# HGRN2 head outputs turned by VectorE through DRAM instead of by TensorE

## The chip, the cores and the metric

The kernel runs on one core of a Trainium2 chip. The metric is device microseconds of one execution, lower is better. The engines are named as the profile names them: PE (TensorE), DVE (VectorE), ACT (ScalarE), POOL (GpSimd) and SP (SyncE, which only issues transfers here); PEld is the load of PE's stationary operand.

## The reference

One layer over 2112 tokens: 2048 of a prompt and 64 of a second, decoded sequence with a state of its own. D is 1024, there are 8 heads of 128. Cut to what matters:

```python
h = rms_norm(x, g_pre)
vA, bA, cA, zA, q, f, iv, zB, gA, gB = split_cols(h @ w_in)        # ten products of 1024
yA = (silu(zA) * bA * causal_conv3(cA * vA, conv_w)) @ w_a_out     # path A
fg = lb + (1 - lb) * sigmoid(f); kk = 1 - fg; qq = silu(q) * 128 ** -0.5
# path B: per head, chunks of 64 tokens, b = cumsum(log fg) within the chunk
att = causal(qe @ ke.T)                  # qe = q exp(b - ref), ke = k exp(ref - b)
o = att @ v + (q * exp(b)) @ S
S = exp(b_last) * S + (k * exp(b_last - b)).T @ v
o = o * rsqrt(mean(o * o) + EPS)         # over the head's 128 channels
yB = ((o * g_onorm) * silu(zB)) @ w_b_out
x = x + rms_norm((sigmoid(gA) * yA + sigmoid(gB) * yB) @ w_o, g_post)
x = x + (p @ w_ple_proj) * sigmoid(rms_norm(x, g_ple) @ w_ple_gate)
```

The mean over a head's channels is along a row of `o` when tokens lie on the partitions; the product with `silu(zB)` and `w_b_out` needs channels on the partitions. So the normalised outputs have to be turned, 128x128 at a time. So have keys and values, which the products over tokens need with tokens on the partitions.

## The kernel before, in words

The tokens are worked through in three blocks of 768, 704 and 640. Block 1 holds the decoded sequence as a half group of 64 tokens. In a block the order is: path B (eight heads), path A, the merge of both, the product with `w_o`, the norm, the last gate. Activations stand with channels on the partitions and tokens on the free axis. Activations and weights are split into a high and a low part in a rounded format, so that a product is three matmuls for each piece of 128 of the contraction (L442, L443, L444).

The large products go through `sgroup` (L427): two output tiles of 128 channels at once, in seven products of a Strassen-Winograd scheme over half the contraction and half the tokens (`PRODUCTS`). Its weights are the blocks of `w_in` and their sums S1 to S4. Block 0 makes these sums (`combined`, additions L352), splits each into halves (ACT casts the high one, DVE subtracts for the low one, L226) and stores what later blocks read again. For weights that only later stages of block 0 need, `prepare_sums` (L364) makes sums ahead, in pieces: load on POOL's queue, an addition on DVE (`keep`, L390), a store on POOL's queue (L393), and the low half (L226, stored by L387).

`sgroup` calls `hook()` once after each of its seven products. `hooks` is a list of steps of other work; each call takes the next entry, which may be None. That sets how work is interleaved: `head_prep` (L936) runs two `sgroup`s for one head, the forget gate with the values and then the output gate zB with the queries, that is 14 hooks, and in them run the attention steps of the head before. In block 0 every head after the first is followed by one `sgroup` of the gates gA and gB (`next(fills)`), which makes 21 hooks a head; in blocks 1 and 2 only one head is.

Within `head_prep` the values (all blocks) and, in blocks 1 and 2, the keys are turned by a round trip. `turned` (L1045): DVE transposes 32x32 squares (L1049), POOL's queue writes the tile to DRAM (L1051). `in_rows` (L1053): POOL's queue reads it back in an order that completes the turn (L1056), and for keys POOL copies it once more into plain columns (L1061).

`head_attn` (L1064) is a generator with four steps for a part of a head, up to four pairs of chunks (a pair is a group of 128 tokens). A block of 768 has the parts 4 + 2, one of 640 has 4 + 1, block 1 has the half group beside these:
1. in block 0, and for the half group, PE transposes the keys (L1093) into PSUM and ACT copies them out (L1095); then the scores on PE (L1121) and their masking on DVE;
2. products of keys and values for the state, and the states;
3. the outputs on PE (L1161, L1163), their squares and the norm, to a tile `on`;
4. PE transposes the pairs back (L1179), and one DVE instruction a part multiplies them, out of PSUM, with `g_onorm` and the gate tile `z` (L1181), in place in `z`.

Then `keep_z` (L1191) stores `z` to DRAM on POOL's queue; the merge reads it later. The query tile's product with the decay factors, `queries`, is on POOL in block 0 (L1017) and on DVE else (L1016). Evictions of `sgroup` stand on ACT (L456) and DVE (L462, L471, L490). Each engine runs its instructions in the order in which they are issued, and so does each queue's issuing engine. Tiles of 128 x up to 770 come from one pool, `ring`, of 48 buffers.

Of the kernel before, what the change touches and what calls it, by code (L numbers as in the profile page):

```python
# [93 lines left out]
def hybrid_step(  # L94
# [266 lines left out]
            total("S4", a12, s2, ALU.subtract)  # L361
            return out

    def prepare_sums(firsts, shared=False, pieces=False):  # L364

        def second(i1):
            return i1 + (KH if i1 >= W_A else 1)  # L370

        def tile_of(dt=F32):
            return rt(4 * P, dt).rearrange("p (k c) -> p k c", c=P)

        def load(i1):
# [12 lines left out]

        def keep(name, i1, out, x, y, op):
            V.tensor_tensor(out, x, y, op)  # L390
# [542 lines left out]
    def chunks(t):  # L933
        return t.rearrange("p (c t) -> p c t", t=CH)

    def head_prep(bl, hc, hd, first, hs):  # L936
        n, npair = bl["n"], bl["npair"]
        nch, np1 = n // CH, npair * P
        sf, vt = rt(), rt()
# [29 lines left out]
        def scaled(after):  # L969


            with tc.issue_after(after):
                if first:
                    A.activation(sf, sf, AF.Identity, bias=omlb[:, hd : hd + 1], scale=nomlb[:, hd : hd + 1])
                A.activation(r, ref.rearrange("p c o -> p (c o)"), AF.Exp)
                A.activation(eq, lg, AF.Exp)
                A.activation(lg, lg, AF.Exp, scale=-1.0)
            V.tensor_tensor(f[:, 1:nch], r[:, 1:nch], chunks(eq)[:, : nch - 1, CH - 1], ALU.mult)
            V.tensor_copy(f[:, 0:1], r[:, 0:1])
            for g in bl["groups"]:  # L980
                if g["sample"]:
                    c = g["off"] // CH
                    V.tensor_copy(f[:, c : c + 1], r[:, c : c + 1])
            f1, f2 = f[:, 0 : 2 * npair : 2], f[:, 1 : 2 * npair : 2]

            ka3 = ka.rearrange("p (g t) -> p g t", t=CH)
            more = npair - 2 * SWAP
            for lo, hi, to in (
                (0, SWAP, ka3[:, more + 1 :: 2, :]),
                (SWAP, 2 * SWAP, ka3[:, more : npair - 1 : 2, :]),  # L990
                (2 * SWAP, npair, ka3[:, :more, :]),
            ):
                own = slice(2 * lo, 2 * hi, 2)
                V.tensor_tensor(to, chunks(sf)[:, own, :], chunks(lg)[:, own, :], ALU.mult)
                scale = f2[:, lo:hi].unsqueeze(2).to_broadcast([P, hi - lo, CH])
                place = slice(2 * lo + (hi <= SWAP), 2 * hi, 2)
                V.tensor_tensor(chunks(kb)[:, place, :], to, scale, ALU.mult)
            for lo, hi in ((0, SWAP), (SWAP, npair)):
                seconds, place = slice(2 * lo + 1, 2 * hi, 2), slice(2 * lo + (hi > SWAP), 2 * hi, 2)
                V.tensor_tensor(chunks(kb)[:, place, :], chunks(sf)[:, seconds, :], chunks(lg)[:, seconds, :], ALU.mult)  # L1000
            if not first:
                wrote.append(turned("tk", kb, b, npair))
            if nch % 2:
                end = slice(nch - 1, nch)
                V.tensor_tensor(chunks(kb)[:, end, :], chunks(sf)[:, end, :], chunks(lg)[:, end, :], ALU.mult)
            V.tensor_tensor(f2, f2, f1, ALU.mult)
# [12 lines left out]
        def sink_q(c, h, x, y):  # L1019
# [4 lines left out]
            else:  # L1024
                v = whole(x, y)
                A.activation(half(z, h), v, AF.Sigmoid)
                V.tensor_tensor(half(z, h), v, half(z, h), ALU.mult)

        with behind_all(summed[-1] if first and hd == 0 else ()):
            sgroup(ZB * 8 + hd, QQ * 8 + hd, hc, sink_q, first, mid=scaled, free=first)  # L1030
        with tc.issue_after(freed[0]) if first else nullcontext():
            queries()
        with behind_all([*wrote, *powers]):
            by_token = [in_rows(kind, npair) for kind in (("tv",) if first else ("tv", "tk"))][::-1]
        return dict(
            eq=eq, f=f, ka=ka, kb=kb, qe=qe, qx=qx, vt=vt, z=z, by_token=by_token,
            more=npair - 2 * SWAP, first=first, last=bl["last"], carry=None,
        )

    def cols3(t, nt):  # L1040
# [9 lines left out]
        turning[kind] = dram.tile([P, n], F32, tag=f"{kind}{npair}", name=nm(kind), bufs=2)  # L1050
        return G.dma_start(turning[kind], out[:, :n]).ins  # L1051

    def in_rows(kind, npair):  # L1053

        t = rt(npair * P)
        G.dma_start(t.rearrange("q (i c) -> q i c", i=4), turning[kind].rearrange("(i b) (j c) -> (b j) i c", i=4, j=4))  # L1056
        t = t.rearrange("q (i g a) -> q g i a", i=4, a=32)
        if kind == "tv":
            return t
        kt = rt(npair * P)  # L1060
        G.tensor_copy(kt.rearrange("q (g i a) -> q g i a", i=4, a=32), t)  # L1061
# [2 lines left out]
    def head_attn(ip, gs, d, hd):  # L1064
# [93 lines left out]
        with placed():  # L1158
            for i, g in enumerate(gs):
                dst = p_o[:, i * P : i * P + P]  # L1160
                T.matmul(dst, att[:, i, :], v[:, i], start=True, stop=prevs[i] is None)  # L1161
                if prevs[i] is not None:
                    T.matmul(dst, cols(d["qx"], g), prevs[i], start=False, stop=True)  # L1163
        on = tile3(2)
        ms = small.tile([P, 4], F32, tag="ms", name=nm("ms"))
        po3 = cols3(p_o, nt)
        if d["first"]:
# [10 lines left out]
            for i in range(nt):  # L1178
                T.transpose(p_t[:, i * P : i * P + P], on[:, i, :], ident)  # L1179
        c = slice(o0, o0 + n)  # L1180
        V.scalar_tensor_tensor(z[:, c], p_t[:, P - ln : P - ln + n], g_on[:, hd : hd + 1], z[:, c], ALU.mult, ALU.mult)  # L1181
        yield

    def each(steps):
        for step in steps:
            step()

    def path_b(bl, hc, first, kept, fills, hs, lead_sums=None):


        def keep_z(hd, z):  # L1191
            kept["o", hd] = spill("o", hd)
            G.dma_start(kept["o", hd], z)

        for hd in range(NH):
            d = head_prep(bl, hc, hd, first, hs)
            if hd > 0 if first else hd == KH + 1:
                next(fills, None)
            assert not hooks
            lead = first and hd == 0  # L1200
            attn = [head_attn(i, gs, d, hd) for i, gs in enumerate(bl["parts"])]
            hooks.extend([None] * (1 + lead if first else 2))
            if not first:
                pairs, one = attn[:2], attn[2:]
                piece = lead_sums and [partial(next, lead_sums, None)]
                for steps in (pairs[:1], pairs[1:], one, one, pairs, one, pairs, piece, one, pairs[:1], pairs[1:]):
                    hooks.append(partial(each, [s if callable(s) else partial(next, s) for s in steps]) if steps else None)
            for step in range(4 * first):
                hooks.extend(partial(next, g) for g in attn)

                hooks.extend([None] * (0 if step == 3 else 3 - len(attn) - (lead and step == 0) + (step == 2)))
            hooks.append(partial(keep_z, hd, d["z"]))
            if first:
                piece = partial(next, lead_sums, None)
                hooks.extend([piece, None, piece, None, piece] if hd else [None, piece])
        if first:
            hooks.extend([None, None, None, piece] * 12)


    parked = []  # L1220
# [375 lines left out]
    for bi, bl in enumerate(blocks):  # L1596
# [145 lines left out]
```

## Time and profile before

| | |
|---|---|
| time, median of three runs | 2563.28 us (2561.38, 2563.28, 2568.24) |
| the profiled execution | 2561.54 us, of which the span of the profile is 2559.8 |
| granted clock of PE | 0.999 |
| ACT, share of the span | 1485.7 us, 58% |
| POOL, share of the span | 451.0 us, 18% |
| the commonest transfer: weights of 256 KB, issued by SP | 577 times, 4.5 us to landing |

The page gives the busy time of each engine, the span in 40 slices, the transfers by kind, the chain of work that ended last, and groups of instructions by line. L12 is line 12 of the kernel; lines of the kernel before are meant unless it is said otherwise. Many instructions run one behind another with overlap, so a duration is not the time that one more instruction costs; that is read from the distance of starts in the timeline.

### The profile page before, as it was taken

What the parts mean: (1) busy time and instruction counts of PE and PEld (TensorE: products, weight loads), DVE (VectorE), ACT (ScalarE), POOL (GpSimd) and SP (SyncE); (2) the same over time, 40 slices, a digit from 0 to 9 for tenths busy, and PEclk for the clock granted to TensorE, in tenths of its full rate; (3) what the DMA queues carried; (4) which work ended last, traced back from release to release, by engine and by line L of the source; (5) the groups of instructions that cost most, each with busy time, mean ns of one, the idle gap of its engine ahead of it and who ended that gap; (6) DMA issues with size and microseconds to landing.
All of it is one profiled execution on the core that took longest, in us unless ns stands there. A gap on an engine that the chain in (4) does not pass through costs nothing.

```text
span 2559.8 us, 47168 instructions
## 1 busy us (share of the span) xinstructions
PE 2540.1 (99%) x16150; PEld 2525.1 (99%) x16150; DVE 1778.2 (69%) x3541; ACT 1485.7 (58%) x2880; POOL 451.0 (18%) x781
## 2 busy tenths in 40 slices
PE   9999999999999999999999999999999999999999
PEld 9999999999999999999999999999999999999998
DVE  7888888898868775576574556987446655336967
ACT  6666666554453664466565555567456665446675
POOL 2122122220022021122221221102112111001011
PEclk9999999999999999999999999999999999999999
DMA  8789888998797888988888999989998898999986
GB/s 330 256 272 321 275 285 287 329 368 300 257 345 249 266 315 263 304 279 285 309 271 290 342 392 314 324 292 334 296 306 299 294 317 288 298 299 324 338 271 202
DMA packets 368400, 767.11 MB, mean 300 GB/s; under 512 B 45398, under 2 KB 50192, under 8 KB 368160
## 3 DMA queue, kind: packets, MB, share of 16 engines
q1 hardware_dynamic: 321696, 582.69, 67.2%
q0 software_dynamic: 46464, 181.41, 19.8%
q8 instruction: 127, 2.08, 0.3%
q14 instruction: 113, 0.93, 0.1%
HBM read 557.07 MB, written 206.85 MB: 298 GB/s over the span
## 4 chain that ended last, share of the span: by engine, by line
PE 76%; issue 3%; DVE 3%; DMA 3%; ACT 1%; POOL 0%; SPq 0%; DVEq 0%; ACTq 0%; POOLq 0%
PE pg L442 16%; PE pg L444 16%; PE pg L443 16%; PE pg L594 4%; PE pg L593 4%; PE pg L595 4%; PE pg L633 3%; PE pg L632 3%; PE pg L631 3%; DMA lo<-low 1%; DMA raw<-w_blk 1%; PE pa L1121 1%; PE pa L1161 1%; PE pa L1163 1%; PE pa L1107 1%
## 5 line engine op out<-in xcount | busy, mean ns | idle before, releaser
L442 PE MATMUL pg<-r,hi 128*128 128x320 f32 (+2 forms) x3304 | 1084.0, 328 | 0.0
L443 PE MATMUL pg<-r,hi 128*128 128x320 f32 (+2 forms) x3304 | 1067.7, 323 | 0.0
L444 PE MATMUL pg<-r,lo 128*128 128x384 f32 (+2 forms) x2356 | 768.8, 326 | 4.3 <-DMA lo<-low 4.1
L273 ACT CAST hi<-raw 128x512 fp32r<-128x512 f32 x730 | 449.9, 619 | 493.5 <-PE pg L443 185.6
L442 PEld LDWEIGHTS pg<-r,hi 128*128 128x128 f32 x3304 | 621.8, 188 | 0.7
L443 PEld LDWEIGHTS pg<-r,hi 128*128 128x128 f32 x3304 | 622.2, 188 | 0.0
L444 PEld LDWEIGHTS pg<-r,lo 128*128 128x128 f32 x2356 | 442.8, 188 | 6.0 <-DMA lo<-low 5.6
L444 PE MATMUL pg<-r,s 128*128 128x352 f32 (+1 forms) x948 | 300.0, 316 | 1.7 <-DMA s<-low 1.7
L594 PE MATMUL pg<-r,hi 128*128 128x320 f32 (+2 forms) x864 | 277.5, 322 | 0.4 <-DVE r L226 0.2
L593 PE MATMUL pg<-r,hi 128*128 128x320 f32 (+2 forms) x864 | 274.9, 322 | 0.0
L226 ACT CAST hi<-raw 128x512 fp32r<-128x512 f32 x252 | 155.4, 620 | 168.7 <-PE pg L443 47.6
L226 DVE TENSOR_TENSOR r<-r,r 128x320 fp32r<-128x320 f32 (+7 forms) x354 | 208.5, 608 | 50.9 <-ACT r L226 49.7
L226 DVE TENSOR_TENSOR lo<-raw,hi 128x512 fp32r<-128x512 f32 x231 | 160.3, 696 | 81.7 <-ACT hi L226 78.5
L226 ACT CAST r<-r 128x320 fp32r<-128x320 f32 (+7 forms) x354 | 185.3, 557 | 49.4 <-DVE r L390 8.2
L595 PE MATMUL pg<-r,lo 128*128 128x352 f32 (+2 forms) x564 | 180.9, 321 | 0.0
L444 PEld LDWEIGHTS pg<-r,s 128*128 128x128 f32 x948 | 178.8, 189 | 2.2 <-DMA s<-low 2.2
L226 ACT CAST hi<-s 128x512 fp32r<-128x512 f32 x156 | 96.5, 619 | 130.7 <-PE pg L443 101.9
L632 PE MATMUL pg<-r,hi 128*128 128x384 f32 (+2 forms) x512 | 167.1, 327 | 0.2 <-DVE r L226 0.2
L631 PE MATMUL pg<-r,hi 128*128 128x384 f32 (+2 forms) x512 | 165.9, 327 | 0.2 <-ACT hi L273 0.2
L594 PEld LDWEIGHTS pg<-r,hi 128*128 128x128 f32 x864 | 162.1, 188 | 2.2 <-DVE r L226 1.6
L593 PEld LDWEIGHTS pg<-r,hi 128*128 128x128 f32 x864 | 161.3, 188 | 1.4 <-ACT r L226 0.7
L456 ACT COPY hf<-pg 128x352 f32<-128x352 f32 (+2 forms) x354 | 157.2, 446 | 1.0 <-PE pg L444 0.6
(396 smaller groups left out, 4109.4 us busy)
## 6 DMA issues: line engine op xcount, KB each, us to landing
raw<-w_blk SPq DMA_DIRECT2D x577, 256.0 KB, 4.5
raw<-S SPq DMA_DIRECT2D x444, 256.0 KB, 4.4
lo<-low SPq DMA_DIRECT2D x422, 256.0 KB, 4.3
s<-low SPq DMA_DIRECT2D x308, 256.0 KB, 4.4
low<-lo SPq DMA_DIRECT2D x271, 256.0 KB, 4.0
S<-s SPq DMA_DIRECT2D x152, 256.0 KB, 3.8
low<-r POOLq DMA_DIRECT2D x54, 256.0 KB, 5.1
r<-w_blk POOLq DMA_DIRECT2D x52, 256.0 KB, 6.6
```

Of the source, the lines that this page charges most:

```text
L226: return A.copy(hi, src).ins, V.tensor_tensor(lo, src, hi.bitcast(F32), ALU.subtract).ins
L273: A.copy(hi, raw)
L442: add(hi[:, k, :], xhi, start=start and k == 0, stop=False)
L443: add(hi[:, k, :], xlo, start=False, stop=False)
L444: last[0] = add(lo[:, k, :], xhi, start=False, stop=k == KH - 1).ins
L456: copied = A.copy(got[n], ps[bank])
L593: add(hi[:, k, :], xhi, start=start and k == 0, stop=False)
L594: add(hi[:, k, :], xlo, start=False, stop=False)
L595: last[0] = add(lo[:, k, :], xhi, start=False, stop=k == KH - 1).ins
L631: T.matmul(ps, hi[:, k % 4, :], xhi[:, c], start=k == ks[0], stop=False)
L632: T.matmul(ps, hi[:, k % 4, :], xlo[:, c], start=False, stop=False)
L633: last[0] = T.matmul(ps, lo[:, k % 4, :], xhi[:, c], start=False, stop=k == ks[-1]).ins
```

## The change

In four parts.

1. The normalised outputs of whole pairs, in all blocks, no longer go through PE and PSUM. They are written to a tile `on` of the whole head; `turn_o` transposes it on DVE into the head's `kb` tile and writes it to DRAM, `read_o` reads it back into `on`, and `scale_o` multiplies it into `z`: in block 0 four DVE instructions of 192 columns with `g_onorm`, in blocks 1 and 2 one product of 640. There `g_onorm` is multiplied into `z` when `z` is made (`sink_q`). The half group of block 1 is still transposed on PE. In blocks 1 and 2 the read stands ahead of the keys' read in POOL's queue.
2. Block 0's keys are turned by `turned` and `in_rows` as in the other blocks; the read and POOL's copy run at the fourth hook of the gates' `sgroup` (`read_k`), for the first head at the end of `head_prep`.
3. The additions of the sums made ahead during block 0's path B run on POOL (`adder=G`): 24 of 128x512.
4. The hooks are laid out by numbered slots (`slots`, `at`) that may reach into the next head's: in blocks 1 and 2 `scale_o` and `keep_z` stand at slot 21, where a head has 14 slots (21 with a gates' `sgroup`).

In the built programs TensorE has 15523 matmuls before and 15347 after.

```diff
-    def prepare_sums(firsts, shared=False, pieces=False):
+    def prepare_sums(firsts, shared=False, pieces=False, adder=V):
...
         def keep(name, i1, out, x, y, op):
-            V.tensor_tensor(out, x, y, op)
+            adder.tensor_tensor(out, x, y, op)
...
-    def head_prep(bl, hc, hd, first, hs):
+    def head_prep(bl, hc, hd, first, hs, before):
...
-            if not first:
-                wrote.append(turned("tk", kb, b, npair))
+            wrote.append(turned("tk", kb, b, npair))
...
-                V.tensor_tensor(half(z, h), v, half(z, h), ALU.mult)
+                V.scalar_tensor_tensor(half(z, h), v, g_on[:, hd : hd + 1], half(z, h), ALU.mult, ALU.mult)
...
-            by_token = [in_rows(kind, npair) for kind in (("tv",) if first else ("tv", "tk"))][::-1]
+            by_token = [in_rows("tv", npair)]
+            if before is not None and not first:
+                before["ot"] = in_rows("to", npair, before["on"])
+            if not first or before is None:
+                by_token.insert(0, in_rows("tk", npair))
...
-    def in_rows(kind, npair):
+    def in_rows(kind, npair, t=None):
-        t = rt(npair * P)
+        t = rt(npair * P) if t is None else t
...
-        on = tile3(2)
+        if not single:
+            d["on"] = rt(d["npair"] * P) if d["on"] is None else d["on"]
+            on = cols3(d["on"][:, o0:], nt)
+        else:
+            on = tile3(2)
...
-        V.scalar_tensor_tensor(z[:, c], p_t[:, P - ln : P - ln + n], g_on[:, hd : hd + 1], z[:, c], ALU.mult, ALU.mult)
+        V.tensor_tensor(z[:, c], p_t[:, P - ln : P - ln + n], z[:, c], ALU.mult)
...
+    def read_k(d):
+        d["by_token"].insert(0, in_rows("tk", d["npair"]))
+    def turn_o(d):
+        turned("to", d["on"], d["kb"], d["npair"])
+    def read_o(d):
+        if "ot" not in d:
+            d["ot"] = in_rows("to", d["npair"], d["on"])
+    def scale_o(d, hd):
+        z = d["z"][:, : d["npair"] * P].rearrange("q (g i a) -> q g i a", i=4, a=32)
+        if d["first"]:
+            for i in range(4):
+                V.scalar_tensor_tensor(z[:, :, i], d["ot"][:, :, i], g_on[:, hd : hd + 1], z[:, :, i], ALU.mult, ALU.mult)
+        else:
+            V.tensor_tensor(z, d["ot"], z, ALU.mult)
...
+        slots, base, d = {}, 0, None
         for hd in range(NH):
-            d = head_prep(bl, hc, hd, first, hs)
+            d = head_prep(bl, hc, hd, first, hs, d)
+            if len(d["by_token"]) == 1:
+                hooks[3] = partial(read_k, d)
...
+            if first:
+                for g in attn:
+                    for slot in (3, 8, 11) if hd == 0 else (1, 4, 7):
+                        at(slot + (g is attn[1]), g)
+                late = 4 * (hd == 0)
+                at(11 + late, partial(turn_o, d))
+                at(16 + late, partial(read_o, d))
+                at(20 + late, partial(scale_o, d, hd), keep)
+                for slot in (13, 15, 18) if hd else (16,):
+                    at(slot, piece)
...
+            else:
...
+                at(11, partial(turn_o, d))
+                at(14, partial(read_o, d))
+                at(14 + 7, partial(scale_o, d, hd), keep)
+            count = 14 + 7 * (first or hd + 1 == KH + 1) if hd + 1 < NH else 1 + max(slots) - base
+            for slot in range(base, base + count):
+                steps = slots.pop(slot, None)
+                hooks.append(partial(each, steps) if steps else None)
+            base += count
...
-        path_b(bl, hc, first, kept, fills, hs if first else None, ahead_of and prepare_sums(ahead_of, pieces=True))
+        path_b(bl, hc, first, kept, fills, hs if first else None, ahead_of and prepare_sums(ahead_of, pieces=True, adder=G if first else V))
```

More of the change, by code (lines that the diff above doesn't have):

```diff
@@ L1033, in head_prep @@
         with behind_all([*wrote, *powers]):
-            by_token = [in_rows(kind, npair) for kind in (("tv",) if first else ("tv", "tk"))][::-1]
+            by_token = [in_rows("tv", npair)]
[3 more added lines that the diff above has]
+                by_token.insert(0, in_rows("tk", npair))
         return dict(
-            eq=eq, f=f, ka=ka, kb=kb, qe=qe, qx=qx, vt=vt, z=z, by_token=by_token,
-            more=npair - 2 * SWAP, first=first, last=bl["last"], carry=None,
+            eq=eq, f=f, ka=ka, kb=kb, qe=qe, qx=qx, vt=vt, z=z, by_token=by_token, on=None,
+            npair=npair, more=npair - 2 * SWAP, first=first, last=bl["last"], carry=None,
         )
@@ L1051, in turned @@
         return G.dma_start(turning[kind], out[:, :n]).ins
-    def in_rows(kind, npair):
-        t = rt(npair * P)
+    def in_rows(kind, npair, t=None):
+        t = rt(npair * P) if t is None else t
         G.dma_start(t.rearrange("q (i c) -> q i c", i=4), turning[kind].rearrange("(i b) (j c) -> (b j) i c", i=4, j=4))
         t = t.rearrange("q (i g a) -> q g i a", i=4, a=32)
-        if kind == "tv":
+        if kind != "tk":
             return t
@@ L1193, in keep_z @@
             G.dma_start(kept["o", hd], z)
+        slots, base, d = {}, 0, None
         for hd in range(NH):
-            d = head_prep(bl, hc, hd, first, hs)
+            d = head_prep(bl, hc, hd, first, hs, d)
+            if len(d["by_token"]) == 1:
+                assert hooks[3] is None
+                hooks[3] = partial(read_k, d)
             if hd > 0 if first else hd == KH + 1:
@@ L1199, in path_b @@
             assert not hooks
-            lead = first and hd == 0
             attn = [head_attn(i, gs, d, hd) for i, gs in enumerate(bl["parts"])]
-            hooks.extend([None] * (1 + lead if first else 2))
-            if not first:
-                pairs, one = attn[:2], attn[2:]
-                piece = lead_sums and [partial(next, lead_sums, None)]
-                for steps in (pairs[:1], pairs[1:], one, one, pairs, one, pairs, piece, one, pairs[:1], pairs[1:]):
-                    hooks.append(partial(each, [s if callable(s) else partial(next, s) for s in steps]) if steps else None)
@@ L1208, in path_b @@
[L1208 to L1217, printed above, removed]
+            keep = partial(keep_z, hd, d["z"])
@@ new lines, in path_b, with at @@
+            piece = lead_sums and partial(next, lead_sums, None)
+            def at(slot, *steps):
+                slots.setdefault(base + slot, []).extend(s if callable(s) else partial(next, s) for s in steps if s is not None)
+            if first:
[8 more added lines that the diff above has]
+                    at(slot, piece)
+                if hd == NH - 1:
+                    for slot in range(22, 70, 4):
+                        at(slot, piece)
+            else:
+                pairs, one = attn[:2], attn[2:]
+                for slot, steps in enumerate((pairs[:1], pairs[1:], one, one, pairs, one, pairs, (piece,), one)):
+                    at(slot + 2, *steps)
+                at(11, partial(turn_o, d))
+                at(14, partial(read_o, d))
+                at(14 + 7, partial(scale_o, d, hd), keep)
```

## The prediction

> **What bounds the kernel now.** I read first the page's busy times, its DMA total and its chain of work that ended last:
>
> ```profile
> PE 2540.1 (99%) x16150; PEld 2525.1 (99%) x16150; DVE 1778.2 (69%) x3541; ACT 1485.7 (58%) x2880; POOL 451.0 (18%) x781
> ...
> DMA packets 368400, 767.11 MB, mean 300 GB/s; under 512 B 45398, under 2 KB 50192, under 8 KB 368160
> ...
> PE 76%; issue 3%; DVE 3%; DMA 3%; ACT 1%; POOL 0%; SPq 0%; DVEq 0%; ACTq 0%; POOLq 0%
> ```
>
> TensorE (PE) is idle for 2559.8 - 2540.1 = 19.7 us in all, and it carries the chain. What is taken out of its instruction stream shortens the kernel, as long as VectorE (DVE) and the DMAs still deliver in time. How much room they have is read from busy times by stage: most of block 0's heads, a piece of one of them, block 1's path A, and block 2's heads.
>
> ```profile
> 112.00:486.00 374.00, 373.00 (x2304) 371.73 (x2303) 315.96 (x613) 239.37 (x473) 83.28 (x114) 1.00 0.83 287
> 228.00:240.00 12.00, 12.00 (x70) 12.00 (x69) 12.00 (x22) 6.76 (x13) 5.60 (x6) 1.00 0.90 300
> 1400.00:1630.00 230.00, 229.42 (x1422) 228.64 (x1421) 143.27 (x284) 127.22 (x259) 47.81 (x102) 1.00 0.96 343
> 1870.00:2170.00 300.00, 300.00 (x2141) 299.88 (x2140) 181.22 (x432) 184.46 (x326) 51.87 (x82) 1.00 0.89 302
> ```
>
> The columns are PE, weight loads, DVE, ACT, POOL, granted clock, DMA share, GB/s. In block 0 DVE is busy 316 of 374 us, and for stretches (228 to 240) wholly, yet PE does not stop. In block 2 DVE has 119 us of 300 to spare. The DMAs are 83 to 96% busy everywhere.
>
> **PE: what is removed.** Before, every output group is turned back on PE (L1179), and block 0's keys too (L1093). By line, with the shortest, median and longest duration in ns:
>
> ```profile
> L1179 PE MATMUL pa<-ident,r x112: 270/272/274, 121.2 to 2151.2; 128*128 128x128 f32 x112
> L1179 PE MATMUL pa<-ident,one x16: 270/271/272, 1111.3 to 2153.1; 128*128 128x128 f32 x16
> ```
>
> ```profile
> L1093 PE MATMUL pa<-ident,r x64: 270/272/273, 95.6 to 1343.2; 128*128 128x128 f32 x64
> ```
>
> How they lie in PE's stream, by the timeline (start, duration):
>
> ```profile
> 431.15 0.34 PE L444 MATMUL pg<-r,lo 128*128 128x384 f32 x1
> 431.33 0.60 PE L1179 MATMUL pa<-ident,r 128*128 128x128 f32 x4
> 431.68 0.42 PE L442 MATMUL pg<-r,hi 128*128 128x384 f32 x1
> 431.94 0.34 PE L443 MATMUL pg<-r,hi 128*128 128x384 f32 x1
> 432.11 0.34 PE L444 MATMUL pg<-r,lo 128*128 128x384 f32 x1
> 432.29 0.34 PE L442 MATMUL pg<-r,hi 128*128 128x384 f32 x1
> ```
>
> The 112 + 16 transposes of whole pairs go; of the 64, 6 x 8 heads = 48 go and the 16 of block 1's half group stay. That is 176. Each lasts 0.27 us, but they overlap: from the product at 431.15 over four transposes to the second product behind them (431.94) is 0.79 us, while two steps without transposes (431.94 to 432.29) are 0.35. Four cost 0.44, one 0.11 us. So PE loses 176 x 0.11 = 19.4 us: 12 x 8 x 0.11 = 10.6 in block 0, 5 x 8 x 0.11 = 4.4 in each of blocks 1 and 2. The Trainium skill (TensorE: Matmul & The Clock Gate, Part 4) gives some 275 ns for a transpose inside a kernel. The trace agrees on the duration, 272 ns; by that rule as a price the change would bring 48 us, by the pitch of the rows 19.4. I take the pitch; the other price is a rival below.
>
> **VectorE.** The prices of what it gains and loses, again by line:
>
> ```profile
> L1049 DVE STREAM_TRANSPOSE r<-r x40: 1304/1329/1605, 76.1 to 2122.6; 128x640 f32<-128x640 f32 x32, 128x768 f32<-128x768 f32 x8
> ```
>
> ```profile
> L1181 DVE SCALAR_TENSOR_TENSOR r<-pa,vec,r x56: 276/474/764, 125.6 to 2153.7; 128x512 f32<-128x512 f32 x24, 128x128 f32<-128x128 f32 x16, 128x256 f32<-128x256 f32 x8, 128x64 f32<-128x64 f32 x8
> ```
>
> ```profile
> L1016 DVE TENSOR_TENSOR r<-r,r x16: 817/851/886, 1081.7 to 2127.7; 128x704 f32<-128x704 f32 x8, 128x640 f32<-128x640 f32 x8
> ```
>
> ```profile
> L390 DVE TENSOR_TENSOR r<-r,r x52: 671/683/693, 184.2 to 1510.2; 128x512 f32<-128x512 f32 x52
> ```
>
> A turn is 1.33 us at 640 columns and 1.6 at 768. L1181's shortest is the 64-wide one (0.28), its median the 256-wide (0.47), its longest the 512-wide (0.76); between 64 and 256 that makes 0.34 at 128 columns and 0.41 at 192. A head of blocks 1 and 2 gains a turn (1.33) and a product of 640 (0.82) and loses two L1181 (0.76 + 0.34): +1.1 us, beside the 119 idle us of block 2. A head of block 0 gains two turns (3.2) and four scalings of 192 (4 x 0.41 = 1.6), and loses 0.76 + 0.47: +3.6 us. Seven heads in the 374 us stage add 25 us, so DVE would be busy 341 of 365 us, 93%. The cover is the distance at which DVE works ahead of PE. I paired the 130 low halves (L226) from 163 to 480 us with PE's groups of four L444, by the smallest shift at which none is used before it is made. The nearest pair:
>
> ```profile
> 343.18 0.68 DVE L226 TENSOR_TENSOR lo<-s,hi 128x512 fp32r<-128x512 f32 x1
> ...
> 344.93 0.34 PE L444 MATMUL pg<-r,lo 128*128 128x384 f32 x1
> ```
>
> It is made at 343.86 and used 1.07 us later; so a delay of about 1 us is covered everywhere. Block 0's price lies between 0 and 8 x 3.6 = 29 us; a gain beyond PE's own is excluded, since PE idles only 1.0 us there. I take 3, close to the lower end, because 12 us of a wholly busy DVE (228 to 240) cost PE nothing.
>
> **The sums on GpSimd (POOL).** 24 additions of 0.68 us leave DVE. POOL's one product of this kind shows what that is worth:
>
> ```profile
> 185.85 3.00 POOL L1017 TENSOR_TENSOR r<-r,qc 128x768 f32<-128x768 f32 x1 [0.17 <-DVE r L1011]
> ...
> 187.90 1.50 DVE L352 TENSOR_TENSOR s<-s,raw 128x512 f32<-128x512 f32 x1
> ```
>
> The bracket tells what ended its idle time. While POOL runs its 768 columns, a DVE instruction of the size of L390's 0.68 takes 1.50: 0.8 us lost, or 0.55 by 512 columns. An addition moved frees 0.13 us of DVE, not 0.68; I count nothing. The Trainium skill says so (GPSIMD Engine Reference, 8. Key points): GpSimd shares its SBUF interfaces with VectorE and contends with DVE instructions that have two SBUF inputs. The row agrees. Behind an addition on POOL, ACT's cast and DVE's subtraction that make the sum's halves wait for it, and on DVE the low halves of the weights stand behind that subtraction; POOL's own stores (L387, L393) and its reads of keys and outputs queue too. The addition's 0.68 on DVE against up to 3.00 x 512/768 = 2.0 on POOL makes at most 1.3 us of waiting, of which the 1 us covers most. POOL also copies block 0's keys (L1061, 768 columns a head): taken as long as the product above, that costs DVE at most 0.8 us a head, 6 in all, and ACT is rid of the two evictions of L1095. All this is part of block 0's price.
>
> **The round trip.** Times to landing:
>
> ```profile
> tv<-r POOLq DMA_DIRECT2D x16, 320.0 KB, 4.0
> tk<-r POOLq DMA_DIRECT2D x16, 320.0 KB, 4.7
> r<-tv POOLq DMA_DIRECT2D x16, 320.0 KB, 6.4
> ...
> tv<-r POOLq DMA_DIRECT2D x8, 384.0 KB, 4.1
> r<-tv POOLq DMA_DIRECT2D x8, 384.0 KB, 4.7
> ```
>
> Traffic: 16 heads x 2 x 320 KB and 8 x 4 x 384 KB, 23 MB on 767. In block 2, 5 MB in 300 us lifts 302 GB/s to about 320, in block 0, 11 MB in 374 us lifts 287 to about 320; the row of 1400 to 1630 carries 343 with PE at 229.4 of 230. I price it at nothing by itself.
>
> Waits: in blocks 1 and 2 the outputs come back 1.33 + 4.0 + 6.4 = 11.7 us after the turn begins. In the built order, 65 matmuls lie between the turn and DVE's product with z, 9 us at 300/2141 us each. DVE will stand there some 3 us per head, with the evictions L471 and L462 and the masks queued behind it. 119 idle us of DVE hide that; uncovered it would be 3 x 15 = 45 us at most, and I take 0. In block 0 it is 1.6 + 4.1 + 4.7 = 10.4 us against 78 matmuls, 12.7 us at 374/2304: no wait. Block 0's keys are read five hook slots before their use, 5 x 374/(7 x 21) = 12.7 us, and need 4.7 and POOL's copy, under 1: no wait either.
>
> The keys of block 2 are closer: POOL's copy, then PE's L1121 that needs it (L1124 in the changed kernel).
>
> ```profile
> 1942.97 0.72 POOL L1061 COPY r<-r 128x640 f32<-128x640 f32 x1 [6.40 <-DMA r<-tk]
> ...
> 1944.32 0.83 PE L1121 MATMUL pa<-r,r 128*128 128x128 f32 x6
> ```
>
> 0.63 us lie between 1943.69 and 1944.32. Afterwards PE arrives 0.55 us earlier (five transposes), the keys' turn stands behind the outputs' (up to 1.33 later), and the keys' read is queued behind one more read (up to 6.4 - 4.0 = 2.4). Per head 0 to 3.6 us, for seven heads 0 to 25. I take 4, nearer to the lower end, since DVE's idle time takes up most of the 1.33 and the reads overlap.
>
> **Sum.** The profiled execution took 2561.5 us: 2561.5 - 19.4 + 3 + 4 = 2549.1. The median of the runs is 1.7 above that execution, so I predict 2551. With the waits between 0 and 13 us its own range is 2544 to 2556.
>
> **Rivals.**
> - *The keys of block 2 come late, or the DMAs crowd*: PE waits before L1121, 9 to 25 us in all in place of the 4 above, and the time is 2556 to 2572, about the same. For it: 0.63 us of room and a DMA share near 0.9. Against: 343 GB/s are carried elsewhere without a stop. Chance 0.21 ("the same", within 0.3% or 7.7 us, is also what a measurement of this kernel can't tell from no change).
> - *VectorE becomes block 0's bound* and the kernel gets slower: each head's 3.6 us reach PE once DVE falls behind by more than its lead, 8 x 3.6 = 29 us, with up to 6 us from POOL's copies: 2563.3 - 19.4 + 29 to 35 = 2573 to 2579. For it: 93% busy and 12 us without a gap already. Against: DVE still has idle time in each head to catch up in. It decides from about 2.5 us of stall per head on. Chance 0.17.
> - *A transpose costs its whole duration*: 176 x 0.272 = 47.9 us off, 2515. The steps at 431 speak against it. Chance 0.02.
> - *The change does not do what it says* is excluded for the transposes, which the built order no longer has.
>
> **How the numbers follow.** The forecast has 0.60. Faster by over 0.3% (below 2555.6): 0.60 + 0.02 = 0.62; the same 0.21; slower 0.17. The range runs from 2543 to 2568: the forecast's own and most of the first rival, leaving out about 0.2.
>
> **What would show it.** In the profile after: PE with 176 fewer matmuls and about 2520 us busy; L1179 only for the half group; the 374 us stage some 10 us shorter with DVE above 90%; idle PE before L1121 in block 2 of a few us in all, with POOL's copy as its releaser; DVE waiting for a DMA at its product with z, 2 to 4 us per head in blocks 1 and 2 with PE still at full. I am wrong if PE idles by more than 15 us more in block 0 (released by DVE or ACT low halves), or if its idle time before L1121 eats the 8.8 us that blocks 1 and 2 bring.

## The result and the profile after

The changed kernel takes 2593.63 us (median of 5 runs, 2589.58 to 2596.64) against 2563.28: 1.0113 times the time before, 95% interval 1.0102 to 1.0125. That is 29 us slower by this ratio (the two medians differ by 30), where 2551 was forecast and 2543 to 2568 given as the range. Rows of the kernel after, and of every run, carry that kernel's own line numbers. The page's first row, its DMA total and its chain:

```profile
PE 2539.2 (98%) x15974; PEld 2513.6 (97%) x15974; DVE 1831.5 (71%) x3549; ACT 1471.8 (57%) x2864; POOL 526.4 (20%) x877
...
DMA packets 374288, 790.17 MB, mean 305 GB/s; under 512 B 46422, under 2 KB 51472, under 8 KB 374048
...
PE 39%; DVE 2%; issue 2%; DMA 2%; ACT 0%; POOL 0%; SPq 0%; ACTq 0%; DVEq 0%; POOLq 0%
```

The span is 2591.9 us, so PE is idle 52.7 us instead of 19.7. Its 176 transposes are gone, yet its busy time is only 0.9 us shorter: other matmuls have become longer. Where the time went is read from when the same stage starts in both kernels. Two groups of L594, in the merges, by line, of the kernel before and of the one after:

```profile
L594 PE MATMUL pg<-r,hi x864: 302/322/442, 694.2 to 2477.8; 128*128 128x320 f32 x67, 128*128 128x352 f32 x64, 128*128 128x384 f32 x42
L594 PE MATMUL pa<-r,hi x32: 320/336/428, 846.2 to 1696.1; 128*128 128x384 f32 x16, 128*128 128x352 f32 x16
```

```profile
L594 PE MATMUL pg<-r,hi x864: 302/322/433, 724.4 to 2509.8; 128*128 128x320 f32 x67, 128*128 128x352 f32 x64, 128*128 128x384 f32 x42
L594 PE MATMUL pa<-r,hi x32: 320/336/431, 875.9 to 1730.5; 128*128 128x384 f32 x16, 128*128 128x352 f32 x16
```

When block 0's first merge begins, 30.2 us are lost; at the end of block 1, 34.4; near the end of the kernel, 32.0. Block 0 makes nearly all of it, block 1 adds some 4, block 2 gives 2 back. The windows of block 0 that were shown of before, and what PE waited for from 50 to 700 us (in total, times, longest):

```profile
112.00:486.00 374.00, 356.89 (x2123) 348.86 (x2122) 330.83 (x598) 218.66 (x434) 118.12 (x157) 0.99 0.87 303
228.00:240.00 12.00, 11.59 (x67) 11.27 (x66) 11.25 (x25) 8.62 (x14) 3.50 (x6) 1.00 0.76 256
```

```profile
PE pg L444 <- DVE lo L226: 19.1, 20, 2.2
PE pg L444 <- DVE qc L979: 2.4, 3, 1.2
PE pg L442 <- ACT hi L226: 1.5, 4, 0.7
```

PE now stops 20 times for a low half that DVE makes late; in the kernel before it did not once. The same window of 50 to 720 us, before and after:

```profile
50.00:720.00 670.00, 668.63 (x4008) 666.73 (x4009) 566.18 (x1050) 396.70 (x776) 130.50 (x201) 1.00 0.85 294
```

```profile
50.00:720.00 670.00, 644.02 (x3741) 631.26 (x3740) 580.43 (x1013) 368.14 (x728) 182.61 (x260) 0.99 0.86 301
```

PE idles 24.6 us more in it. The prediction had named more than 15 us, behind late low halves, as the sign that it is wrong. DVE is busy 331 of 374 us, 88%, which is less than the 93% that was forecast: it is late because it stands and because its instructions are stretched (shown below), and not because it is full.

A stop can cost more than its idle time. Windows of the kernel after around one of 2.0 us, with the granted clock before the last two columns:

```profile
260.00:262.00 2.00, 0.64 (x4) 0.32 (x2) 2.00 (x2) 0.49 (x2) 1.92 (x2) 1.00 0.99 366
262.00:264.00 2.00, 1.38 (x7) 1.38 (x7) 2.00 (x4) 0.32 (x1) 0.55 (x2) 0.88 0.68 186
264.00:266.00 2.00, 2.00 (x9) 2.00 (x9) 1.87 (x5) 2.00 (x5) 1.87 (x3) 0.50 0.76 292
266.00:268.00 2.00, 2.00 (x12) 2.00 (x12) 2.00 (x5) 0.83 (x2) 0.00 (x0) 0.77 0.89 314
```

Behind this stop PE runs at a granted clock of 0.50, reached only after it had already gone on for a microsecond. The three windows from 262 on lose 2 x (0.12 + 0.50 + 0.23) = 1.7 us. Summed over windows of 25 us the dips of the clock take 12 us of the change's span and 2 of the span before, up to the kernel's last 25 us. These 10 us are more than half of what kept PE's busy time where it was.

### The profile page after: what moved, and what is told of

It reads as the page before. It is cut to its first block, busy times and chain, and to the rows that moved or that the text cites. A ratio compares the mean times of both kernels' runs of the same rounds, so it can differ in the third digit from the quotient of the medians.

```text
span 2591.9 us, 46906 instructions
## 1 busy us (share of the span) xinstructions
PE 2539.2 (98%) x15974; PEld 2513.6 (97%) x15974; DVE 1831.5 (71%) x3549; ACT 1471.8 (57%) x2864; POOL 526.4 (20%) x877
## 5 line engine op out<-in xcount | busy, mean ns | idle before, releaser
L444 PE MATMUL pg<-r,lo 128*128 128x384 f32 (+2 forms) x2356 | 774.2, 329 | 23.1 <-DVE lo L226 19.1
L444 PEld LDWEIGHTS pg<-r,lo 128*128 128x128 f32 x2356 | 444.7, 189 | 33.0 <-DVE lo L226 29.5
L444 PE MATMUL pg<-r,s 128*128 128x352 f32 (+1 forms) x948 | 300.2, 317 | 1.3 <-DMA s<-low 1.3
L594 PE MATMUL pg<-r,hi 128*128 128x320 f32 (+2 forms) x864 | 277.3, 322 | 0.3 <-DVE r L226 0.2
L226 ACT CAST r<-r 128x320 fp32r<-128x320 f32 (+7 forms) x354 | 185.7, 557 | 58.2 <-POOL r L390 14.1
L444 PEld LDWEIGHTS pg<-r,s 128*128 128x128 f32 x948 | 178.6, 188 | 1.7 <-DMA s<-low 1.7
L594 PEld LDWEIGHTS pg<-r,hi 128*128 128x128 f32 x864 | 162.1, 188 | 2.1 <-DVE r L226 1.6
```

What stands on the lines that cost most here:

```text
L226: return A.copy(hi, src).ins, V.tensor_tensor(lo, src, hi.bitcast(F32), ALU.subtract).ins
L444: last[0] = add(lo[:, k, :], xhi, start=False, stop=k == KH - 1).ins
L594: add(hi[:, k, :], xlo, start=False, stop=False)
```

## The experiments

Each version was timed in five rounds against the kernel before. All were built from the changed kernel, with switches that set the other parts back to what they were before; the edits below are shown in essence. "us" is the ratio's distance from 1 times 2564, the kernel before.

| run | what differs | ratio (95% interval) | us |
|---|---|---|---|
| the change | | 1.0113 (1.0102 to 1.0125) | +29 |
| e1 | change, additions on VectorE | 1.0052 (1.0039 to 1.0064) | +13.3 |
| e2 | before, additions on GpSimd | 1.0090 (1.0076 to 1.0103) | +23.1 |
| e3 | change in blocks 1 and 2 only | 1.0002 (0.9993 to 1.0011) | +0.5 |
| e4 | e3 and block 0's outputs | 1.0025 (1.0014 to 1.0035) | +6.4 |
| e5 | before, 24 additions more on GpSimd, unused | 1.0039 (1.0025 to 1.0052) | +10.0 |
| e6 | before, unused transfers in block 0 | 1.0017 (1.0008 to 1.0026) | +4.4 |
| e7 | before, unused turns in block 0 | 1.0030 (1.0018 to 1.0041) | +7.7 |
| e8 | e3 and block 0's keys | 1.0018 (1.0006 to 1.0030) | +4.6 |
| e9 | e3, block 1's sums earlier | 0.9984 (0.9975 to 0.9992) | -4.1 |
| e10 | outputs in block 2 only | 0.9983 (0.9974 to 0.9992) | -4.4 |
| e11 | e2 with nobody waiting for the sums | 1.0017 (1.0009 to 1.0026) | +4.4 |
| e12 | before, 136 transposes more | 1.0048 (1.0035 to 1.0062) | +12.3 |
| e13 | e1, block 0's product held back | 1.0014 (1.0003 to 1.0025) | +3.6 |
| e14 | before, e6 and e7 at once | 1.0043 (1.0028 to 1.0058) | +11.0 |

**The additions on GpSimd: e1, e2, e5, e11.** The theory (A) was that they are the main loss, the rival (B) that VectorE's added turns are. e1 takes them back, e2 does them alone:

```diff
-... prepare_sums(ahead_of, pieces=True, adder=G if first else V)
+... prepare_sums(ahead_of, pieces=True, adder=V)          # e1, in the changed kernel
-... prepare_sums(ahead_of, pieces=True)
+... prepare_sums(ahead_of, pieces=True, adder=G if first else V)   # e2, in the kernel before
```

> The changed kernel with block 0's 24 additions ahead back on VectorE (adder=V); all else as changed. Theory A (GpSimd's additions stretch VectorE's instructions beside them by 25 us in all where moving them saves 16, and hold up GpSimd's queue): most of block 0's loss goes, 2593.6 falls by 15 to 30, to 2564 to 2579. Theory B (block 0 is lost to VectorE's added turns and scalings, about 3.6 us a head, whatever the additions do): VectorE gets 16 us more to do, 2594 to 2605. If PE idles in block 0 behind low halves less than in the changed kernel (19 us), A has it.

> The kernel before with one edit: block 0's 24 additions ahead on GpSimd. Theory A: PE waits for low halves that VectorE delivers late, 2563.3 + 10 to 25 = 2573 to 2588. Theory B: VectorE has room enough without the turns, 2563 within 4.

e1 wins back 15.6 of the 29 us, close to the least that A allowed; e2 loses 23.1, which only A allows. The 13.3 us that e1 still loses are not explained by A. How an addition costs is seen in the change's own timeline, first DVE, then POOL:

```profile
355.46 1.96 DVE L226 TENSOR_TENSOR lo<-s,hi 128x512 fp32r<-128x512 f32 x1
357.34 1.80 DVE L471 TENSOR_TENSOR hf<-hf,hf 128x384 f32<-128x384 f32 x1
...
362.49 2.08 DVE L352 TENSOR_TENSOR s<-raw,s 128x512 f32<-128x512 f32 x1
```

```profile
355.15 1.72 POOL L1016 TENSOR_TENSOR r<-r,qc 128x768 f32<-128x768 f32 x1
356.82 0.58 POOL L387 DMA_DIRECT2D low<-r  x1
357.42 1.30 POOL L390 TENSOR_TENSOR r<-r,r 128x512 f32<-128x512 f32 x1
...
362.71 1.30 POOL L390 TENSOR_TENSOR r<-r,r 128x512 f32<-128x512 f32 x1
```

DVE's instruction of 0.68 us takes 2.08 beside POOL's addition, one of 0.55 takes 1.80: it is held up for about as long as POOL's runs. Where two instructions of POOL follow one another it gets worse. DVE, POOL and PE, some 110 us later:

```profile
463.07 3.47 DVE L471 TENSOR_TENSOR hf<-hf,hf 128x384 f32<-128x384 f32 x1
...
467.07 0.68 DVE L226 TENSOR_TENSOR lo<-raw,hi 128x512 fp32r<-128x512 f32 x1
```

```profile
463.40 1.49 POOL L1016 TENSOR_TENSOR r<-r,qc 128x768 f32<-128x768 f32 x1
464.84 1.28 POOL L390 TENSOR_TENSOR r<-r,r 128x512 f32<-128x512 f32 x1
```

```profile
467.80 0.44 PE L444 MATMUL pg<-r,lo 128*128 128x384 f32 x1 [2.23 <-DVE lo L226]
```

An instruction of 0.55 us takes 3.47, the low half behind it is late, and PE stops 2.23 us. Nine of PE's 20 stops for low halves last over 1 us. Two of them stand behind DVE's wait at the product with `z` (below); in the 5 us before each of the other seven, DVE has an instruction of 0.55 to 0.69 us that took 1.79 to 3.47 beside POOL's work. So the move does not free DVE. In e2's page DVE is busier than the 1778.2 us of the kernel before:

```profile
PE 2551.3 (99%) x16150; PEld 2533.1 (98%) x16150; DVE 1792.1 (69%) x3517; ACT 1484.3 (57%) x2880; POOL 483.6 (19%) x805
```

That is 13.9 us more, though 24 x 0.68 = 16.3 us of additions have left it: by this sum each addition on POOL costs DVE some 1.26 us. e5 and e11 divide the stretching from the waiting for the sums. e5 adds 24 additions that nobody waits for; e11 moves them, but lets everything behind go on without the sum:

```diff
+    def extra_add():                                       # e5, at the pieces' hooks
+        G.tensor_tensor(rt(4 * P), keep[:, : 4 * P], keep[:, : 4 * P], ALU.add)
-            adder.tensor_tensor(out, x, y, op)
+            G.tensor_tensor(tile_of(), ones, ones, op)     # e11, block 0's
```

> The kernel before plus 24 additions of 128x512 on GpSimd in block 0, at the hooks of the real ones, on constant data and into tiles that nothing reads; the real additions stay on VectorE. Nobody waits for the extra ones. Theory A1 (the additions cost by stretching VectorE's instructions that run beside them): most of the 23 us that the real move cost comes back here, 2564.6 + 8 to 25 = 2573 to 2590. Theory A2 (they cost because ScalarE's casts and VectorE's subtractions queue behind the slower sum, and the key evictions and low halves behind those): 2564.6 within 4.

> The kernel before with block 0's 24 additions ahead taken off VectorE and as many on GpSimd, on constant data and into tiles that nothing reads; what follows each sum (cast, low half, stores) works on the unsummed tile, so the sums ahead are left out. Against the real move (2587.7) only the waiting for GpSimd's sums is gone. Theory A1 (stretching of VectorE's instructions): as far as the dummies went, +9 less what 16 us of freed VectorE are worth, 2564 + 3 to 10 = 2567 to 2574, and the other 14 to 20 us of the real move are waits for the sums. If the waits cost nothing: 2580 to 2588.

Both parts of A are real. Additions that nobody waits for cost 10.0 with DVE's own additions kept, and 4.4 net when these are gone; some of that may be the time that they take in POOL's queue, which these runs do not part from the stretching. The real move costs 23.1, and DVE is as busy in e11 (1791.4 us) as in e2, so the 18.7 us between them are put down to waiting for the sums. In e2's trace PE's and ACT's waits are these (L1107 there is L1095 of before, L448 is L444, L394 is L390):

```profile
PE pa L1118 <- ACT r L1107: 9.0, 4, 3.0
PE pg L448 <- DVE lo L230: 6.0, 8, 1.9
```

```profile
ACT r L230 <- POOL r L394: 12.9, 6, 3.1
```

ACT, which casts the sum's high half, stands there up to 3.1 us. But PE's four stops for the keys' eviction do not come straight behind this. At each of them ACT has just stood 3.1 to 5.0 us at another place, for an eviction of DVE (L494 there) that comes late behind stretched instructions; before the longest:

```profile
361.30 0.84 ACT L863 ACTIVATE r<-r 128x768 f32<-128x768 f32 x1 [5.00 <-DVE r L494]
```

At three of the four, waits of ACT for a sum, of 1.6 to 3.1 us, lie 12 to 18 us earlier. How they reach PE from there is argued, not shown. In the change block 0's keys have no eviction on ACT, but its casts still stand for the sums. How its 15.6 us divide into waiting and stretching was not tried. From 50 to 720 us of the change:

```profile
ACT r L226 <- POOL r L390: 14.1, 8, 3.7
```

**Outputs and keys in block 0: e4, e8, e6, e7, e13, e14.** e4 and e8 do one of the two:

```diff
-            wrote.append(turned("tk", kb, b, npair))
+            if not first: wrote.append(turned("tk", kb, b, npair))   # e4: no keys; PE turns them
+        trip = not first                                             # e8: no outputs; PE turns them
```

> Outputs by round trip in all blocks, block 0's keys by PE as before and its additions on VectorE. Block 0 sheds 48 transposes (5.3 us at 0.11) and VectorE gains about 2 us a head. Theory A: block 0 at least breaks even, 2560 to 2567. Theory B: half of the turned work is there, so about half of block 0's 41 us of loss: 2573 to 2585.

> Block 0's keys by the round trip, its outputs by PE and its additions on VectorE; outputs by round trip in blocks 1 and 2. On top of the outputs the keys cost 2579.2 - 2569.8 = 9.4. If the two parts only add up: 2565.5 + 9 = 2575. If either fits alone and only both together run over what VectorE and the DMAs have to spare: 2560 to 2568.

Against e3, outputs cost 5.9 us and keys 4.1, together (e1) 12.8: neither half pays, and within their intervals they add up. e4 lies between A and B, e8 between its two branches: more is at work in block 0 than the additions. e6 and e7 put each resource alone into the kernel before:

```diff
+                at(6, partial(extra_write, 0)); at(10, partial(extra_read, 0))      # e6: 384 KB each
+                at(12, partial(extra_write, 1)); at(17, partial(extra_read, 1))
+                at(6, extra_turn); at(12, extra_turn)                               # e7: 128x768 each
```

> The kernel before plus, for each head of block 0, two writes of 128x768 to DRAM and two reads in the round trip's order on GpSimd's queue, on constant data, nobody waiting for them but the queue. No VectorE work is added. Theory C (the round trip's transfers crowd the DMAs: VectorE waits for low-half stores to land before it can reuse the buffer, 19 to 25 us in the changed kernels against 4): 2564.6 + 8 to 20 = 2573 to 2585. Theory D (VectorE's own added work is what costs): 2564.6 within 4.

> The kernel before plus two VectorE transposes of 128x768 for each head of block 0, of constant data into tiles that nothing reads: 16 x 1.59 = 25 us more on VectorE, no transfers, no waits. Theory D: PE stops behind late low halves, 2564.6 + 8 to 25 = 2573 to 2590. Theory C: VectorE had 58 idle us in this stage and takes it, 2564.6 within 4.

> The kernel before plus both dummies in block 0 at once: two turns of constant data a head on VectorE and the two writes and reads. Alone they cost +8 and +4. If the costs only add up (theory I): 2564 + 12 = 2576. If each uses up the slack that hides the other (theory J): 2564 + 16 to 25 = 2580 to 2589, which would account for the 22 us that outputs and keys together cost in block 0 before what PE saves.

The transfers cost 4.4 us, just above what D gave and far from C. They lengthen DVE's wait for the stores of low halves, from the first row, of the kernel before, to the second, of e6:

```profile
DVE lo L226 <- DMA low<-lo: 3.8, 2, 2.5
```

```profile
DVE lo L230 <- DMA low<-lo: 21.3, 14, 3.3
```

Most of that stays without effect on PE: in the profiled execution of e6, one of its faster ones with 2564.35 us, PE is only some 1 us more idle from 50 to 720 us, so its trace does not show where the 4.4 us go. POOL's queue also stands 66.5 us there for the dummies' own reads, which belongs to the price. The turns cost 7.7 us for 25 us of work, just short of D's range and outside C's. PE does not wait for low halves there, as D had it, but for DVE's masking of the scores, in e7:

```profile
PE pa L1125 <- DVE att L1134: 5.1, 3, 2.8
```

So e7 gives what such work costs at the hooks where it stands; in the change the same work delays other instructions. Together (e14) they cost 11.0: they add up (I), J falls. That left about 10 us open. In the trace of the change, POOL, DVE and PE around the first head's outputs:

```profile
133.49 0.55 POOL L1054 DMA_DIRECT2D to<-r  x1 [0.16 <-issue]
140.68 0.82 POOL L1064 COPY r<-r 128x768 f32<-128x768 f32 x1 [6.64 <-DMA r<-tk]
141.48 1.46 POOL L1016 TENSOR_TENSOR r<-r,qc 128x768 f32<-128x768 f32 x1
142.89 0.81 POOL L1059 DMA_DIRECT2D r<-to  x1
```

```profile
147.67 0.42 DVE L1209 SCALAR_TENSOR_TENSOR r<-r,vec,r 128x192 f32<-128x192 f32 x1 [6.56 <-DMA r<-to]
```

```profile
148.75 0.45 PE L444 MATMUL pg<-r,lo 128*128 128x384 f32 x1 [1.53 <-DVE lo L226]
```

The outputs are written at 133.5, but their read stands in POOL's queue behind the copy of keys that are still on their way, and is issued 9 us later. DVE stands 6.56 us at the product, the low halves queued behind it are late, and PE stops. The other wait of this kind is the last head's, and it has another reason:

```profile
503.99 0.78 POOL L1059 DMA_DIRECT2D r<-to  x1 [2.72 <-DMA to<-r]
```

```profile
510.31 0.42 DVE L1209 SCALAR_TENSOR_TENSOR r<-r,vec,r 128x192 f32<-128x192 f32 x1 [4.90 <-DMA r<-to]
```

```profile
511.38 0.44 PE L444 MATMUL pg<-r,lo 128*128 128x384 f32 x1 [2.01 <-DVE lo L226]
```

Here no copy stands ahead of the read, which only waits for the write. The trip takes 11.4 us from the start of the turn (498.88), but DVE is at the product 6.5 us after it. 37 matmuls start in that time; in the first head it is 54, in the six others, where DVE does not stand, 74 to 99. e1 has the same two waits:

```profile
DVE r L1221 <- DMA r<-to: 12.6, 2, 6.5
```

e13 holds that product back on DVE:

```diff
-                at(20 + late, partial(scale_o, d, hd), keep)
+                at(25 + late, partial(scale_o, d, hd), keep)
...
-                V.scalar_tensor_tensor(z[:, :, i], ...)
+                with tc.issue_after(adds[0]):
+                    V.scalar_tensor_tensor(z[:, :, i], ...)
```

> The kernel of e1 (outputs and keys by round trip, additions on VectorE) with block 0's product of the returned outputs with the gate held back on VectorE by some 20 instructions. In e1 VectorE stood 12.6 us at that product for the outputs' read, twice over 6 us, because the read is queued on GpSimd behind the copy of keys that themselves are still on their way. Theory G (these stops make the low halves late): 2579 - 5 to 12 = 2567 to 2574. Theory H (what counts is the sum of VectorE's work and of waits for stores, the stops are taken out of slack): 2576 to 2581.

13.3 becomes 3.6 us: G holds, the two stops at this product were worth 10.

**Blocks 1 and 2: e3, e9, e10.**

```diff
+TURNED = (1, 2)        # e3, e9: block 0 as before; (2,) in e10
-                for slot, steps in enumerate((pairs[:1], pairs[1:], one, one, pairs, one, pairs, (piece,), one)):
+                for slot, steps in enumerate((pairs[:1], pairs[1:], one, one, pairs, one, pairs, (), one)):
+                at(6, piece)                                                   # e9
```

> The changed kernel with block 0's outputs, keys, additions and hooks as before; only blocks 1 and 2 take the round trip for outputs. Both theories: block 0 loses nothing, and what is left is what the two traces show for blocks 1 and 2, +4.7 and -2.4 us: 2563.3 + 2.3 = 2565.6, with VectorE's wait for a weight load in block 1's second head and PE's 5.3 us stop behind it still there. If blocks 1 and 2 suffered only from block 0's late start (states or stores in the queue), 2555 to 2558.

> Block 0 as before, outputs by round trip in blocks 1 and 2, and block 1's sums ahead taken from hook slot 9 of a head to slot 6, so that their loads stand ahead of the outputs' write in GpSimd's queue and their additions ahead of the queries on VectorE. Theory E (block 1's loss is this one stop: the loads queue behind a write that waits for the turn, VectorE waits for the loads, PE for the queries, 5 us, and then runs at half clock for some us): 2565.5 - 5 to 8 = 2557 to 2560. Theory F (blocks 1 and 2 lose in many small places what the transposes bring): 2563 to 2566.

> The kernel before with the outputs' round trip in block 2 alone, where the traces showed 2.4 us of gain: 40 transposes fewer, 4.4 us by their pitch. Theory E: 2564 - 2.4 to 4.4 = 2559 to 2562. Theory F, or keys that come late in block 2: 2564 or more.

e3 comes out even with the kernel before, within its interval as expected. The largest part of its loss is in one place, in the change too. POOL, DVE, and PE's wait in the trace after:

```profile
1133.66 0.60 POOL L1054 DMA_DIRECT2D to<-r  x1 [2.08 <-DVE r L1052]
1134.26 1.61 POOL L379 DMA_DIRECT2D r<-w_blk  x3
```

```profile
1141.91 0.69 DVE L390 TENSOR_TENSOR r<-r,r 128x512 f32<-128x512 f32 x1 [3.42 <-issue]
```

```profile
PE pa L1109 <- DVE r L1015: 5.3, 1, 5.3
```

The loads of block 1's sums ahead are queued on POOL behind the outputs' write, which waits for DVE's turn; DVE's addition waits for the loads, the queries (L1015) for DVE, PE 5.3 us for the queries. e9 takes the loads out of that place and gains 4.6 us over e3: E's time, and not F's. e9 and e10 are the two versions here that beat the kernel before, by 0.16 and 0.17%: small, but clear of zero. That block 2 alone gives as much as both together means block 1 still loses about what its transposes bring; where, was not tried.

**The price of a transpose: e12.**

```diff
-            for i in range(nt):
+            for i in [*range(nt)] * 2:
                 T.transpose(p_t[:, i * P : i * P + P], on[:, i, :], ident)
```

> The kernel before with every output transpose on PE done twice into the same place: 136 more. It measures the price of a transpose. By the pitch of 0.11 us: 2564 + 15 = 2579. By their duration of 0.272 us: 2564 + 37 = 2601. If PE had hidden slack for them: under 2570.

136 more cost 12.3 us (9 to 16): 0.09 each (0.07 to 0.12), near the pitch of 0.11 and far from the duration:

```profile
L1195 PE MATMUL pa<-ident,r x224: 269/273/273, 121.8 to 2162.3; 128*128 128x128 f32 x112
```

## Why the prediction was wrong, point by point

- **PE, -19.4 us.** Right in kind and slightly large: 176 x 0.09 = 16 us. The duration as price is excluded by e12.
- **Block 0's price, 3 us.** This is the step that failed. It was put close to 0 from a range that ended at 29; block 0 came out 30 us later, 39 before what PE saved in it. In its place the runs show 16 us for the sums on POOL, 10 for the two stops at block 0's product, 8 for the turns and 4 for the transfers. VectorE's added work was sized right (turns 25 us, products 3, that is 3.5 us a head against 3.6), and it cost 7.7 us rather than 3. A wholly busy DVE from 228 to 240 was no evidence for its cover: it showed a stretch in which the work fitted, not one in which it was late.
- **"No wait" at block 0's product.** Wrong in two heads of eight, about 10 us. The round trip of 10.4 us was set against 78 matmuls, which is about right for the six heads between. In the first head the read's place in POOL's queue, behind a copy that itself waits for a transfer, was not counted; in the last one the trip took 11.4 us and only 37 matmuls lie in front of the product.
- **The sums on GpSimd, nothing.** Wrong, 16 us of the 29. An addition moved does not free 0.13 us of DVE: it costs some 1.26 and saves 0.68. The one row that the 0.55 rested on is not typical: there POOL's product was stretched as well (3.00 us, against 1.72 at 355.15 above) and DVE lost only 0.8, while beside POOL's additions it loses about their whole 1.3 us. The waiting of at most 1.3 us was too small too: ACT stood up to 3.7 us for a sum, 14.1 in all, since POOL's queue ahead of an addition was not counted.
- **Traffic, nothing by itself.** Too low: e6 gives 4.4 us with a DMA share of 0.90 in the stage. DVE's buffers for low halves come free later there; that this is the way to PE is not shown.
- **Waits in blocks 1 and 2.** Half right. DVE stood at its product with z for 25.8 us in 8 places of block 1 and for this in block 2, 2.8 to 3.2 us a head as forecast:

```profile
DVE r L1211 <- DMA r<-to: 22.7, 8, 7.3
```

  In block 2 that cost nothing visible. In block 1 the write ahead of the loads, a queue that was not looked at, cost 4.6.
- **Block 2's keys, 4 us.** Too high; PE waited twice:

```profile
PE pa L1124 <- POOL r L1064: 1.1, 2, 0.8
```

- **The rival that VectorE becomes block 0's bound** (0.17) came nearest: PE is released by late low halves, as it said. But its time, 2573 to 2579, was 15 to 21 us too low, and its price, 29 to 35 us of DVE's work reaching PE in full, is not what was paid. The work cost 8, the sums 16, the stops at the product 10, the transfers 4, which makes 38; less 9 for block 0's 96 transposes it is 29, beside the 30.2 of the traces. The 16 and the 10 are differences of versions of the change. What they leave, e13 less e3, is 3.1, and 8 + 4 - 9 from the dummies is 3. The terms have intervals of 2 to 4 us each, and the dummies delay other instructions than the change does, so that the sum closes this closely is in part luck.

## What to carry to other kernels

A read or a write that is put on a queue is priced by what stands ahead of it there: here loads behind a write that waits for a turn cost 4.6 us, and a read behind a copy that waits for a transfer is one of two stops that cost 10, and neither shows in the diff. A cover that is counted in the middle of a loop is counted again for its first and last pass. Moving elementwise work to GpSimd is judged by who waits for its result on every engine, and by whether VectorE is freed at all: here it was busier afterwards. The cheap test of an engine's slack is to put unused work of the same kind into the kernel and time it, though it prices only the places where that work is put: 25 us of turns cost 8, 24 additions 10, 12 MB of transfers 4.

## What the hardware showed that was not expected

A stop of PE of 2.0 us was followed by a granted clock of 0.50 for about 3 us, 1.7 us lost on top (262 to 268 us above). The Trainium skill (TensorE: Matmul & The Clock Gate, Part 1, What's actually happening) has the clock halve after an idle window of about 3.4 us; here a stop of 2.0 us was enough, so the trace does not agree with that length. Nor does the length of one stop decide it. Behind a stop of 2.24 us in the same stage the clock stays at 1.00:

```profile
197.00 0.44 PE L444 MATMUL pg<-r,lo 128*128 128x384 f32 x1 [2.24 <-DVE lo L226]
```

```profile
198.00:200.00 2.00, 2.00 (x13) 2.00 (x12) 2.00 (x3) 1.99 (x5) 1.35 (x2) 1.00 0.99 157
```

A VectorE instruction with two inputs in SBUF beside an addition on GpSimd took 2.08 us instead of 0.68, so it was held for about the whole 1.30 us of the addition. e5's 24 additions, which touch nothing of the kernel's data, cost 10 us, by this and by their time in GpSimd's queue.
